# Decoder trunk on one core: the second branch's sums of y formed during the gates and kept in DRAM, one tanh moved, both adds of m ahead of the splits

## The chip, the core and the metric

One core of a Trainium2 chip runs the whole program. The core has five engines that work side by side, each through its own list of instructions in order: TensorE (PE, matrix products), VectorE (DVE), ScalarE (ACT), GpSimd (POOL) and SyncE (SP), which here only issues DMA transfers. SBUF is the on-chip memory, PSUM the small memory into which PE writes its products, and DRAM (HBM) lies outside. The metric is the device time of one execution in microseconds (us); smaller is better.

## What is computed

One layer of a decoder trunk on 1024 positions and 1024 channels, in float32. The part that matters here is the merge of two token mixers:

```python
h = rmsnorm(x, mix_norm[l])
proj = h @ w_in[l]
q, k, v, su, sv, g_a, g_b = jnp.split(proj, splits, axis=-1)
y_att = sliding_window_attention(q, k, v, q_norm[l], k_norm[l], sinks[l])
y_sgu = chunked_spatial_gating(su, sv, sgu_norm[l], w_s[l], b_s[l])
merged = (jax.nn.sigmoid(g_a) * (y_att @ w_oa[l])
          + jax.nn.sigmoid(g_b) * (y_sgu @ w_ob[l]))
x = x + merged @ w_out[l]
x = x + conv_gated_mlp(rmsnorm(x, ffn_norm[l]), w_up[l], conv_w[l], conv_b[l], w_down[l])
```

## The kernel before

**Stages.** The program runs in this order: load and attention (to about 200 us), the spatial gating unit, the *gates* (g_a and g_b, eight pairs of column tiles, to about 380 us), the two branch products with the merge (the *units*, about 380 to 480 us), the product with w_out (to about 560 us), and the MLP.

**Arithmetic.** PE's fast float32 path drops low bits, so each operand is split into a high part (a copy by ACT into type fp32r, `copy_hi`, line 89) and a low part (operand minus high part, on DVE or POOL), and a product is three matmuls: high by high, high by low, low by high. On top of this the large products use a scheme of seven block products instead of eight: the right operand, here y, is cut into four blocks B11, B12, B21, B22, and sums T1 to T4 of these blocks are formed; the seven products are A11·B11, S3·T3, A12·B21, S1·T1, A22·T4, S2·T2 and S4·B22. T1 = B11 - B12, T3 = B12 - B22, T2 = -T1 - B22, T4 = B21 + T2.

**The two y.** Branch "b" is the gating unit, and its y lies in SBUF as `uT`. Branch "a" is attention, and its y lies in DRAM (`d_ya`) and is loaded by `ya_load` into the tile `ya`. `y_sum` (from line 1186) forms one sum of a branch; `y_split` (line 1200) splits one block or sum into the tiles y0 to y6. The sums of "b" are formed in the gates, one for each pair c = 3 to 6 (`gate_pair`); those of "a" are formed in place in `ya`, by `a_begin`, at the end of unit 0.

**The gates.** `gate_pair(c, prev)` makes columns c of g_b and g_a: seven products of 12 matmuls each, with the loads and splits of the weights of the next pair between them. Each gate is scaled (line 1076), goes through tanh on ACT (`gate_out`, line 1089) into a tile `th`, and is stored to DRAM (`dth`), since SBUF has no room for all sixteen.

**The units.** Eight units, in the order of `B_UNITS`: b0, b1, a0, b2, a1, b3, a2, a3. Here they are called unit 0 to unit 7. Unit u is two jobs: the first has the products A11·B11, S3·T3, A12·B21, S1·T1, the second A22·T4, S2·T2, S4·B22, of 6 matmuls each. In between, in this order on each engine:

- ACT copies the first product out of PSUM (`x1`, line 1287), since A12·B21 is added onto the same PSUM bank, and then S3·T3 (`x7`, line 1289). A12·B21 waits for `x1`.
- `hooks` (u, 0) and (u, 1) are pieces of work for branch "a" that are put behind the first and the second job of a unit; the hook "end" (`gates_end`) stands in the first job of unit 0, behind its copies.
- In the second job DVE adds x1 (line 1308), ACT copies the result to `u2` (line 1309), and DVE forms the rest.
- The result times (1 + tanh) goes to a tile `m` for branch "b" (line 1321), and in place for "a" (line 1323). For branch "a" `m_add` then adds it to m (line 1342) and splits m into `mh` and `ml`; it runs behind the first job of the next unit (`late`).
- `run_jobs` splits the weights of job i + 2 (`branch_split`: `wjh` on ACT, line 89, and `wjl` on POOL, line 1273) and loads those of job i + 4 while job i runs; `th_load(u + 1)` loads the two gates of the next unit.

All of this stands in program order (`manual_schedule`), so the order of the lists is the order of the code. Tiles of one tag share a slot or a ring of slots; a new tile waits until the old one's readers are done.

Of the kernel before, what the change touches and what calls it, by code (L numbers as in the profile page):

```python
# [41 lines left out]
def body(ctx, tc, nc, a):  # L42
# [1058 lines left out]
    def gates_close():  # L1101
        pools["gp_cm"].__exit__(None, None, None)
        zr_cm[0].__exit__(None, None, None)
        del pools["AX"]
        pools["mg_cm"] = tc.tile_pool(name="mg", bufs=1)
        pools["mg"] = pools["mg_cm"].__enter__()
        pools["mr_cm"] = tc.tile_pool(name="mr", bufs=1, side="right", reuse_waits="tile")
        pools["mr"] = pools["mr_cm"].__enter__()
        pools["mh0"] = pools["mr"].tile([128, 4, 1024], R, name="mh0")
        pools["mr"].tile([128, 96], F, name="pad_m")  # L1110

    def gate_pair(c, prev):
        w = g_left[c]
        nx = g_left[c + 1] if c < 7 else None
        q = Blocks(w.w, xb)
        x1, x7, q.u2 = q.temps()
        prev.last_sum()
        q.prod(q.g0, "A11", "B11")
        if nx:
            nx.load_q()  # L1120
        else:
            job_load(0)
            job_load(1)
        nc.scalar.copy(x1, q.g0)
        if c == 1:
            gate_out(("a", 0), prev.zv)
        w.split_r()
        gate_out(("b", c - 1), prev.zg)
        if nx:
            wb_add(c - 1)  # L1130
        if 2 < c < 7:
            y_sum("b", ("T1", "T3", "T2", "T4")[c - 3])
        q.prod(q.v0, "S3", "T3")
        nc.scalar.copy(x7, q.v0)
        if not nx:
            y_split("b", "B11")
            y_split("b", "T3")
        q.prod(q.g0, "A12", "B21", more=True)
        if nx:
            nx.sums_q()  # L1140
            nx.split_p()
            nx.split_s3()
        else:
            job_split(0)
            job_load(2)
        q.prod(q.g1, "S1", "T1")
        sub(nc.vector, x7, x7, q.g1)
        if nx:
            nx.sums_r()
        else:  # L1150
            y_split("b", "B21")
            y_split("b", "T1")
        q.prod(q.v0, "A22", "T4", more=True)
        if nx:
            nx.split_q()
        else:
            job_split(1)
        if c == 5:
            ya_load()
        if c < 6:  # L1160
            g_left[c + 2].load_p()
        q.prod(q.v1, "S2", "T2")
        q.sums(x1, x7, q.v0)
        if not nx:
            y_split("b", "T4")
            y_split("b", "T2")
            job_load(3)
        gate_out(("a", c), q.zv)
        q.prod(q.g1, "S4", "B22", more=True)
        if not nx:  # L1170
            y_split("b", "B22")
        return q
# [12 lines left out]

    def y_sum(br, n):

        into = {"a": {"T1": "B11", "T3": "B12", "T2": "B22", "T4": "B21"}, "b": {"T4": "B12"}}[br].get(n)
        if into:
            out = y_src(br, into)  # L1190
        else:
            out = pools["ls"].tile([128, 2, 512], F, tag="m", name=nm("yt"), bufs=3)
        x, y = {"T1": ("B11", "B12"), "T3": ("B12", "B22"), "T2": ("T1", "B22"), "T4": ("B21", "T2")}[n]
        x, y = y_src(br, x), y_src(br, y)
        if n == "T2":
            neg_sum(out, x, y)
        else:
            sub(nc.vector, out, x, y, ALU.add if n == "T4" else ALU.subtract)
        y_raw[br, n] = out

    def y_split(br, n, eng=nc.vector):
        i, j = Y_PLACE[br + n]
# [12 lines left out]
    def gates():  # L1215
        q = v_end()
        for c in range(1, 8):
            q = gate_pair(c, q)
        un["hooks"]["end"] = lambda: gates_end(q)
        un["hooks"][0, 0] = lambda: [y_split("a", n) for n in ("B11", "B22", "B21")]  # L1220
        un["hooks"][0, 1] = a_begin
        un["hooks"][1, 0] = a_end

    def gates_end(q):
        q.last_sum()
        gate_out(("b", 7), q.zg)
        gates_close()
        th_load(0)

    def a_begin():  # L1230
        for n in ("T1", "T3", "T2", "T4"):
            y_sum("a", n)
        y_split("a", "T3")
        y_split("a", "T1")

    def a_end():
        y_split("a", "T4")
        y_split("a", "T2", nc.gpsimd)

    B_UNITS = [("b", 0), ("b", 1), ("a", 0), ("b", 2), ("a", 1), ("b", 3), ("a", 2), ("a", 3)]  # L1240
    ms = {}
# [91 lines left out]
    def m_add(u, j, q):  # L1333

        i = j // 2
        if mhi[i] is None:
            mhi[i] = Y("mh") if i else pools["mh0"]
            mlo[i] = Y("ml")
        for e, z in enumerate((q.zg, q.zv)):
            c = 2 * j + e  # L1340
            m, h, l = ms.pop(c), mhi[i][:, c % 4, :], mlo[i][:, c % 4, :]
            nc.vector.tensor_tensor(m, m, z, op=ALU.add)
            copy_hi(h, m)
            if u == 7 or e == 0:
                nc.vector.tensor_tensor(l, m, h.bitcast(F), op=ALU.subtract)
            else:
                m_lo(m, h, l, L)()
                lo_late.append(m_lo(m, h, l, H))
# [669 lines left out]
```

## Time and profile before

| | us |
|---|---|
| median of three runs | 1202.72 (1202.1 to 1203.13) |
| the profiled execution, its own time | 1203.1 |
| span of its trace (first to last instruction) | 1201.4 |
| PE busy in it | 1173.8 (98%) |
| DVE, ACT, POOL busy | 873.2, 565.6, 620.0 |
| PE busy from 240 to 380 us (gates) | 140.00 of 140 |
| PE busy from 380 to 480 us (units) | 85.06 of 100 |
| PE busy from 580 to 987 us (most of the MLP) | 406.97 of 407 |

The profiled execution is 0.4 us above the median, and 1.7 us of its time lie outside the span. In the rows of a timeline the columns are start, duration, engine, line, operation, output <- inputs by the program's names without buffer numbers, shape, count; in square brackets stands how long the engine had been idle before, and what ended that. PEclk is the clock that PE was granted, 1.00 or 9 in a digit being full speed.

### The profile page before, as it was taken

What the parts mean: (1) busy time and instruction counts of PE and PEld (TensorE: products, weight loads), DVE (VectorE), ACT (ScalarE), POOL (GpSimd) and SP (SyncE); (2) the same over time, 40 slices, a digit from 0 to 9 for tenths busy, and PEclk for the clock granted to TensorE, in tenths of its full rate; (3) what the DMA queues carried; (4) which work ended last, traced back from release to release, by engine and by line L of the source; (5) the groups of instructions that cost most, each with busy time, mean ns of one, the idle gap of its engine ahead of it and who ended that gap; (6) DMA issues with size and microseconds to landing.
All of it is one profiled execution on the core that took longest, in us unless ns stands there. A gap on an engine that the chain in (4) does not pass through costs nothing.

```text
span 1201.4 us, 15911 instructions
## 1 busy us (share of the span) xinstructions
PE 1173.8 (98%) x5842; PEld 991.5 (83%) x5842; DVE 873.2 (73%) x1038; ACT 565.6 (47%) x878; POOL 620.0 (52%) x433
## 2 busy tenths in 40 slices
PE   8999999999999699999999999999999999999998
PEld 8989989888887577788888888888888888888887
DVE  7799966742436767668787878878887798876674
ACT  8555567743336344333644444454444445424331
POOL 2367684588683355344876776767777551000000
PEclk9999999999999799999999999999999999999999
DMA  7010145245654565354564464545545358975471
GB/s 278 26 54 19 53 141 211 89 131 150 174 176 133 172 204 189 92 184 133 130 176 123 140 166 130 155 119 166 142 148 137 100 195 280 368 251 193 146 230 71
DMA packets 79934, 185.51 MB, mean 154 GB/s; under 512 B 9072, under 2 KB 16496, under 8 KB 79728
## 3 DMA queue, kind: packets, MB, share of 16 engines
q1 hardware_dynamic: 72144, 164.57, 40.3%
q0 software_dynamic: 7456, 15.73, 8.4%
q10 hardware_dynamic: 256, 4.19, 1.1%
q8 instruction: 46, 0.75, 0.3%
q14 instruction: 32, 0.26, 0.1%
HBM read 145.40 MB, written 47.45 MB: 161 GB/s over the span
## 4 chain that ended last, share of the span: by engine, by line
PE 59%; DVE 0%; POOL 0%; issue 0%; POOLq 0%
PE pz L1060 35%; PE pd L1832 10%; PE pdy L1832 8%; PE px L95 2%; PE px L94 2%; PE px L93 2%; DVE res L1852 0%; PE pz L140 0%; PE pz L1503 0%; POOL ml L1351 0%; POOL wjl L110 0%; POOLq L110 0%
## 5 line engine op out<-in xcount | busy, mean ns | idle before, releaser
L1060 PE MATMUL pz<-T,qh 128*128 128x512 f32 x472 | 145.6, 390 | 0.0
L1060 PE MATMUL pz<-B,ph 128*128 128x512 f32 x352 | 109.6, 393 | 0.0
L1060 PEld LDWEIGHTS pz<-T,qh 128*128 128x128 f32 x472 | 88.5, 188 | 18.7 <-ACT u L885 0.3
L1019 POOL TENSOR_TENSOR pl<-lp,ph 128x1024 fp32r<-128x1024 f32 x30 | 73.0, 2435 | 52.2 <-ACT ph L89 52.2
L1060 PE MATMUL pz<-T,ql 128*128 128x512 f32 x236 | 91.8, 389 | 0.0
L1060 PE MATMUL pz<-y,wjh 128*128 128x512 f32 x224 | 71.9, 403 | 14.9 <-ACT x L1287 14.8
L1019 POOL TENSOR_TENSOR ql<-lq,qh 128x1024 fp32r<-128x1024 f32 x30 | 76.7, 2556 | 9.1 <-ACT qh L89 9.1
L1060 PEld LDWEIGHTS pz<-B,ph 128*128 128x128 f32 x352 | 65.1, 188 | 15.8 <-ACT x L1672 2.8
L1076 DVE TENSOR_TENSOR pz<-pz,rstd_b 128x1024 f32<-128x1024 f32 x60 | 73.9, 1232 | 4.6 <-ACT rstd_b L143 2.5
L1060 PE MATMUL pz<-T,s3h 128*128 128x512 f32 x232 | 71.4, 389 | 0.0
L1060 PE MATMUL pz<-B,pl 128*128 128x512 f32 x176 | 68.6, 390 | 0.0
L1832 PE MATMUL pd<-bl,ah 128*128 128x512 f32 x176 | 68.5, 389 | 0.0
L1832 PE MATMUL pd<-bh,ah 128*128 128x512 f32 x176 | 68.5, 389 | 0.0
L1832 PE MATMUL pd<-bh,al 128*128 128x512 f32 x176 | 68.5, 389 | 0.0
L1060 PEld LDWEIGHTS pz<-y,wjh 128*128 128x128 f32 x224 | 42.9, 194 | 26.4 <-ACT x L1287 16.5
L1060 PE MATMUL pz<-T,AX 128*128 128x512 f32 x264 | 63.4, 389 | 0.0
L1060 PE MATMUL pz<-B,AX 128*128 128x512 f32 x264 | 63.4, 389 | 0.0
L1273 POOL TENSOR_TENSOR wjl<-wj,wjh 128x512 fp32r<-128x512 f32 (+1 forms) x32 | 36.8, 1170 | 49.2 <-ACT wjh L89 49.2
L622 DVE TENSOR_TENSOR x<-x,pz 128x512 f32<-128x512 f32 x36 | 24.5, 681 | 46.8 <-PE pz L1060 46.8
L1060 PEld LDWEIGHTS pz<-T,AX 128*128 128x128 f32 x264 | 49.6, 188 | 10.3
L1060 PEld LDWEIGHTS pz<-B,AX 128*128 128x128 f32 x264 | 49.6, 188 | 10.3
L1019 POOL TENSOR_TENSOR s3l<-lq,s3h 128x512 fp32r<-128x512 f32 x20 | 25.9, 1297 | 61.5 <-ACT s3h L89 61.5
(353 smaller groups left out, 3601.0 us busy)
## 6 DMA issues: line engine op xcount, KB each, us to landing
lp<-wup SPq DMA_DIRECT2D x22, 512.0 KB, 3.8
lq<-wup SPq DMA_DIRECT2D x22, 512.0 KB, 4.2
ra<-wdown SPq DMA_DIRECT2D x44, 256.0 KB, 4.9
b<-T SPq DMA_DIRECT2D x44, 256.0 KB, 3.5
lq<-wup POOLq DMA_DIRECT2D x42, 256.0 KB, 5.3
B<-tv SPq DMA_DIRECT2D x33, 256.0 KB, 2.0
T<-tt SPq DMA_DIRECT2D x33, 256.0 KB, 2.2
b<-B SPq DMA_DIRECT2D x33, 256.0 KB, 3.0
```

The lines of the kernel that those rows point to most:

```text
L93: nc.tensor.matmul(out, wh, mh, start=first, stop=False, **kw)
L94: nc.tensor.matmul(out, wh, ml, start=False, stop=False, **kw)
L95: nc.tensor.matmul(out, wl, mh, start=False, stop=last, **kw)
L622: eng.tensor_tensor(out, x, y, op=op)
L1019: nc.gpsimd.tensor_tensor(l, r, h.bitcast(F), op=ALU.subtract)
L1060: nc.tensor.matmul(o, p[:, k, :], m, start=not more and k == 0 and j == 0, stop=k == nk - 1 and j == 2, skip_group_check=True)
L1076: nc.vector.tensor_tensor(z, z, rstd_b, op=ALU.mult)
L1273: nc.gpsimd.tensor_tensor(l[:, k], r[:, k], h[:, k].bitcast(F), op=ALU.subtract)
L1832: nc.tensor.matmul(o[d], p[:, k - k0, m], q[:, k - k0, :], start=new and k == 0 and j == 0, stop=k == HK - 1 and j == 2, skip_group_check= ...
```

## The change

The edits, all between the gates and the product with w_out:

1. The sums of branch "a" are formed in the gates. `ya_load` is called in pair c = 1 instead of c = 5, and a table `Y_SUMS` names which sum is made at which of two places of which pair: place 0 is where the sums of "b" stood, place 1 is behind the subtraction of S1·T1 from x7. T3 of "a" is formed in place in `ya`; T1, T2 and T4 are formed in the tiles `yt` (three slots, those that `m` uses later) and stored to DRAM, 512 KB each. Two sums of "b" stay at place 0 and two go to place 1.
2. `ta_load`, at the end of `gates_end`, loads T1, T4 and T2 of "a" from DRAM into a tile `ta`, in the slot in which `mh0` follows later. On SP's list these three loads stand ahead of the gates of unit 0 (`th_load(0)`).
3. The splits of "a" are put elsewhere: behind the first job of unit 0 stand B11 (low part on DVE), B21 and B22 (low parts on POOL, were on DVE), behind its second job T3 and T1, behind the first job of unit 1 T4 and T2 (low part on POOL, as before).
4. The tanh of the last g_a pair (`gate_out(("a", 7))`) goes from the end of the last gate pair to `gates_end`, behind the copies x1 and x7 of unit 0.
5. `m_add` adds both tiles to m before it copies the first high part.

ACT at the start of the units, before (`th` is the tanh of a gate, `y3<-uT` the copy of block B22 of "b", `x1`, `x7`, `u2` the copies of units 0 and 1, `wjh` weights, `y4<-ya` the copies of T3 and T1 of branch "a"; between the two pieces lie weights' high parts and the copies of B11, B22 and B21 of "a"):

```order
L1089 ACTIVATE th_516_4073<-pz_499_3936 128x1024
L89 ACTIVATE y3_518_4089<-uT_59_683 128x1024
L1287 COPY x1_521_4094<-pz_519_4092 128x512
L1289 COPY x7_522_4095<-pz_520_4093 128x512
L1089 ACTIVATE th_524_4125<-pz_498_3935 128x1024
...
L1309 COPY u2_523_4096<-pz_520_4093 128x512
L89 ACTIVATE wjh_535_4192<-wj_515_4069 128x512
L89 ACTIVATE wjh_535_4192<-wj_515_4069 128x256
L89 ACTIVATE y4_539_4207<-ya_476_3764 128x1024 x2
L1287 COPY x1_542_4214<-pz_540_4212 128x512
```

The same place of ACT with the change:

```order
L89 ACTIVATE y3_519_4098<-uT_59_683 128x1024
L1298 COPY x1_522_4103<-pz_520_4101 128x512
L1300 COPY x7_523_4104<-pz_521_4102 128x512
L1089 ACTIVATE th_525_4132<-pz_502_3949 128x1024
L1089 ACTIVATE th_527_4138<-pz_501_3948 128x1024
...
L1320 COPY u2_524_4105<-pz_521_4102 128x512
L89 ACTIVATE wjh_538_4208<-wj_518_4082 128x512
L89 ACTIVATE wjh_538_4208<-wj_518_4082 128x256
L89 ACTIVATE y4_542_4219<-ya_397_3230 128x1024
L89 ACTIVATE y4_542_4219<-ta_4150 128x1024
L1298 COPY x1_545_4226<-pz_543_4224 128x512
```

The first tanh has gone behind x7, and the last of the copies ahead of unit 1's x1 now reads `ta`, which a DMA fills, instead of `ya`.

DVE from the subtraction into x7 of unit 0 to the addition of x1 of unit 1, before (`ya<-ya` are the sums, `y<-ya` the low parts):

```order
L622 TENSOR_TENSOR x7_522_4095<-x7_522_4095,pz_519_4092 128x512
L1208 TENSOR_TENSOR y6_531_4155<-ya_476_3764,y6_531_4155 128x1024 x2
L1208 TENSOR_TENSOR y3_518_4089<-ya_476_3764,y3_518_4089 128x1024
L1308 TENSOR_TENSOR pz_520_4093<-x1_521_4094,pz_520_4093 128x512
...
L1321 SCALAR_TENSOR_TENSOR m_538_4201<-th_527_4141,pz_520_4093 128x1024
L622 TENSOR_TENSOR ya_476_3764<-ya_476_3764 128x2x512 x2
L626 SCALAR_TENSOR_TENSOR ya_476_3764<-ya_476_3764 128x2x512
L622 TENSOR_TENSOR ya_476_3764<-ya_476_3764 128x2x512
L1208 TENSOR_TENSOR y4_539_4207<-ya_476_3764,y4_539_4207 128x1024 x2
L622 TENSOR_TENSOR x7_543_4215<-x7_543_4215,pz_540_4212 128x512
L1208 TENSOR_TENSOR y5_548_4255<-ya_476_3764,y5_548_4255 128x1024
L1308 TENSOR_TENSOR pz_541_4213<-x1_542_4214,pz_541_4213 128x512
```

and with the change:

```order
L622 TENSOR_TENSOR x7_523_4104<-x7_523_4104,pz_520_4101 128x512
L1226 TENSOR_TENSOR y6_534_4171<-ya_397_3230,y6_534_4171 128x1024
L1319 TENSOR_TENSOR pz_521_4102<-x1_522_4103,pz_521_4102 128x512
...
L1332 SCALAR_TENSOR_TENSOR m_541_4217<-th_530_4157,pz_521_4102 128x1024
L1226 TENSOR_TENSOR y4_542_4219<-ya_397_3230,y4_542_4219 128x1024
L1226 TENSOR_TENSOR y4_542_4219<-ta_4150,y4_542_4219 128x1024
L622 TENSOR_TENSOR x7_546_4227<-x7_546_4227,pz_543_4224 128x512
L1226 TENSOR_TENSOR y5_551_4267<-ta_4150,y5_551_4267 128x1024
L1319 TENSOR_TENSOR pz_544_4225<-x1_545_4226,pz_544_4225 128x512
```

The four sums and two of the low parts have left DVE's list here.

SP at the end of the gates with the change (`dth` are the stores of the last two gates, `ta` the new loads, `th` the gates of unit 0, `wj` weights of unit 2):

```order
L1091 DMA dth_526_4134<-th_525_4132 128x1024
L1091 DMA dth_528_4140<-th_527_4138 128x1024
L1216 DMA ta_4150<-taT1_3350 128x1024
L1216 DMA ta_4150<-taT4_3574 128x1024
L1216 DMA ta_4150<-taT2_3487 128x1024
L1262 DMA th_529_4155<-dth_388_3159 128x1024
L1262 DMA th_530_4157<-dth_408_3296 128x1024
L1276 DMA wj_531_4159<-wb 128x256
```

Before, the two `th` loads followed the two stores directly. The diff:

```diff
@@ -1106,8 +1106,6 @@
         pools["mg"] = pools["mg_cm"].__enter__()
         pools["mr_cm"] = tc.tile_pool(name="mr", bufs=1, side="right", reuse_waits="tile")
         pools["mr"] = pools["mr_cm"].__enter__()
-        pools["mh0"] = pools["mr"].tile([128, 4, 1024], R, name="mh0")
-        pools["mr"].tile([128, 96], F, name="pad_m")
 
     def gate_pair(c, prev):
         w = g_left[c]
@@ -1128,8 +1126,7 @@
         gate_out(("b", c - 1), prev.zg)
         if nx:
             wb_add(c - 1)
-        if 2 < c < 7:
-            y_sum("b", ("T1", "T3", "T2", "T4")[c - 3])
+        y_sums(c, 0)
         q.prod(q.v0, "S3", "T3")
         nc.scalar.copy(x7, q.v0)
         if not nx:
@@ -1145,6 +1142,7 @@
             job_load(2)
         q.prod(q.g1, "S1", "T1")
         sub(nc.vector, x7, x7, q.g1)
+        y_sums(c, 1)
         if nx:
             nx.sums_r()
         else:
@@ -1155,7 +1153,7 @@
             nx.split_q()
         else:
             job_split(1)
-        if c == 5:
+        if c == 1:
             ya_load()
         if c < 6:
             g_left[c + 2].load_p()
@@ -1165,7 +1163,8 @@
             y_split("b", "T4")
             y_split("b", "T2")
             job_load(3)
-        gate_out(("a", c), q.zv)
+        if nx:
+            gate_out(("a", c), q.zv)
         q.prod(q.g1, "S4", "B22", more=True)
         if not nx:
             y_split("b", "B22")
@@ -1185,7 +1184,7 @@
 
     def y_sum(br, n):
 
-        into = {"a": {"T1": "B11", "T3": "B12", "T2": "B22", "T4": "B21"}, "b": {"T4": "B12"}}[br].get(n)
+        into = {"a": {"T3": "B12"}, "b": {"T4": "B12"}}[br].get(n)
         if into:
             out = y_src(br, into)
         else:
@@ -1197,6 +1196,25 @@
         else:
             sub(nc.vector, out, x, y, ALU.add if n == "T4" else ALU.subtract)
         y_raw[br, n] = out
+        if br == "a" and n != "T3":
+            d = d_ta[n] = pools["dr"].tile([128, 1024], F, tag=f"ta{n}", name=f"ta{n}")
+            nc.sync.dma_start(d, out.rearrange("p a b -> p (a b)"))
+
+    d_ta = {}
+    Y_SUMS = {(2, 1): "aT1", (3, 0): "aT3", (3, 1): "aT2", (4, 0): "aT4", (4, 1): "bT1", (5, 0): "bT3",
+              (5, 1): "bT2", (6, 0): "bT4"}
+
+    def y_sums(c, e):
+        n = Y_SUMS.get((c, e))
+        if n:
+            y_sum(n[0], n[1:])
+
+    def ta_load():
+        t = pools["mr"].tile([128, 4, 1024], F, tag="mh0", name="ta")
+        pools["mr"].tile([128, 96], F, name="pad_m")
+        for i, n in enumerate(("T1", "T4", "T2")):
+            nc.sync.dma_start(t[:, i, :], d_ta[n])
+            y_raw["a", n] = t[:, i, :].rearrange("p (a b) -> p a b", a=2)
 
     def y_split(br, n, eng=nc.vector):
         i, j = Y_PLACE[br + n]
@@ -1217,25 +1235,18 @@
         for c in range(1, 8):
             q = gate_pair(c, q)
         un["hooks"]["end"] = lambda: gates_end(q)
-        un["hooks"][0, 0] = lambda: [y_split("a", n) for n in ("B11", "B22", "B21")]
-        un["hooks"][0, 1] = a_begin
-        un["hooks"][1, 0] = a_end
+        un["hooks"][0, 0] = lambda: (y_split("a", "B11"), y_split("a", "B21", nc.gpsimd),
+                                     y_split("a", "B22", nc.gpsimd))
+        un["hooks"][0, 1] = lambda: (y_split("a", "T3"), y_split("a", "T1"))
+        un["hooks"][1, 0] = lambda: (y_split("a", "T4"), y_split("a", "T2", nc.gpsimd))
 
     def gates_end(q):
+        gate_out(("a", 7), q.zv)
         q.last_sum()
         gate_out(("b", 7), q.zg)
         gates_close()
+        ta_load()
         th_load(0)
-
-    def a_begin():
-        for n in ("T1", "T3", "T2", "T4"):
-            y_sum("a", n)
-        y_split("a", "T3")
-        y_split("a", "T1")
-
-    def a_end():
-        y_split("a", "T4")
-        y_split("a", "T2", nc.gpsimd)
 
     B_UNITS = [("b", 0), ("b", 1), ("a", 0), ("b", 2), ("a", 1), ("b", 3), ("a", 2), ("a", 3)]
     ms = {}
@@ -1334,12 +1345,14 @@
 
         i = j // 2
         if mhi[i] is None:
-            mhi[i] = Y("mh") if i else pools["mh0"]
+            mhi[i] = Y("mh") if i else pools["mr"].tile([128, 4, 1024], R, tag="mh0", name="mh0")
             mlo[i] = Y("ml")
         for e, z in enumerate((q.zg, q.zv)):
             c = 2 * j + e
+            nc.vector.tensor_tensor(ms[c], ms[c], z, op=ALU.add)
+        for e in (0, 1):
+            c = 2 * j + e
             m, h, l = ms.pop(c), mhi[i][:, c % 4, :], mlo[i][:, c % 4, :]
-            nc.vector.tensor_tensor(m, m, z, op=ALU.add)
             copy_hi(h, m)
             if u == 7 or e == 0:
                 nc.vector.tensor_tensor(l, m, h.bitcast(F), op=ALU.subtract)
```

## The prediction

> **What bounds the kernel now.** I read the page first, then the waits of PE, then the timeline of each engine where PE waits.
>
> ```profile
> span 1201.4 us, 15911 instructions
> ...
> PEclk9999999999999799999999999999999999999999
> ```
>
> PE is the bound nearly everywhere: only what PE loses can be won. The clock digits show one fall, in the fourteenth slice, at about 400 us. The list of waits for PE from 376 to 420 us and from 420 to 480 us names the same line both times (columns: total, count, longest):
>
> ```profile
> PE pz L1060 <- ACT x L1287: 12.4, 2, 11.1
> ```
> ```profile
> PE pz L1060 <- ACT x L1287: 2.4, 2, 1.2
> ```
>
> So 14.8 us go in four waits for one thing, the copy x1 that ACT makes in the first job of a unit. In the timeline of PE the two early ones are these:
>
> ```profile
> 383.78 0.73 PE L1060 MATMUL pz<-y,wjh 128*128 128x512 f32 x2 [1.23 <-ACT x L1287]
> ...
> 393.23 0.39 PE L1060 MATMUL pz<-y,wjl 128*128 128x512 f32 x1
> 404.76 1.22 PE L1060 MATMUL pz<-y,wjh 128*128 128x512 f32 x2 [11.15 <-ACT x L1287]
> ...
> 417.20 0.62 PE L1060 MATMUL pz<-y,wjh 128*128 128x512 f32 x2
> ```
>
> They are the A12·B21 of units 0, 1 and 2; unit 2's came without a wait. After the long wait the matmuls themselves were slow. Stretches of the window view (length, PE, PEld, DVE, ACT, POOL, granted clock):
>
> ```profile
> 404.76:410.70 5.94, 5.93 (x14) 4.68 (x15) 2.58 (x3) 1.23 (x3) 0.08 (x1) 0.50 0.05 19
> 410.70:417.20 6.50, 6.50 (x29) 5.33 (x29) 4.76 (x6) 4.16 (x7) 6.50 (x4) 1.00 0.20 61
> ```
>
> For 5.94 us a matmul took 0.424 us instead of 0.224, so 14 of them cost 14 x 0.200 = 2.8 us more. The long wait is worth 11.15 + 2.8 = 14 us, over 1% of the time.
>
> Why x1 of unit 1 was late, by ACT's timeline:
>
> ```profile
> 381.28 1.03 ACT L1089 ACTIVATE th<-pz 128x1024 f32<-128x1024 f32 x1 [0.86 <-DVE pz L1076]
> 382.21 1.05 ACT L89 ACTIVATE y<-uT 128x1024 fp32r<-128x1024 f32 x1
> 383.15 0.58 ACT L1287 COPY x<-pz 128x512 f32<-128x512 f32 x1
> ...
> 386.55 1.03 ACT L1089 ACTIVATE th<-pz 128x1024 f32<-128x1024 f32 x1 [2.33 <-DVE pz L1076]
> 387.47 1.14 ACT L89 ACTIVATE wjh<-wj 128x512 fp32r<-128x512 f32 x2
> 388.51 2.95 ACT L89 ACTIVATE y<-ya 128x1024 fp32r<-128x1024 f32 x3
> 394.71 0.58 ACT L1309 COPY u<-pz 128x512 f32<-128x512 f32 x1 [3.26 <-DVE pz L1308]
> 395.20 0.94 ACT L89 ACTIVATE wjh<-wj 128x512 fp32r<-128x512 f32 x2
> 402.24 2.00 ACT L89 ACTIVATE y<-ya 128x1024 fp32r<-128x1024 f32 x2 [6.11 <-DVE ya L622]
> 404.15 0.56 ACT L1287 COPY x<-pz 128x512 f32<-128x512 f32 x1
> ```
>
> x1 (404.15) stands behind two copies of branch "a" that waited 6.11 us for sums on DVE, and those behind u2, which waited 3.26 us for DVE's line 1308. DVE at that time:
>
> ```profile
> 389.59 4.48 DVE L1208 TENSOR_TENSOR y<-ya,y 128x1024 fp32r<-128x1024 f32 x3 [1.95 <-ACT y L89]
> 394.00 0.68 DVE L1308 TENSOR_TENSOR pz<-x,pz 128x512 f32<-128x512 f32 x1
> ...
> 397.46 2.35 DVE L1321 SCALAR_TENSOR_TENSOR m<-th,pz 128x1024 f32<-128x1024 f32 x2
> 399.73 2.48 DVE L622 TENSOR_TENSOR ya<-ya 128x1024 f32<-128x1024 f32 x2
> ```
>
> **Unit 0: the tanh behind the copies.** Without the tanh at 381.28 the copy of B22 and x1 (383.15) come up to 1.03 us earlier, x1 ending by 382.8 at the latest. PE was ready at 383.78 - 1.23 = 382.55, so at most 0.3 of this wait stays, and PE comes to unit 1's wait about 1.2 us sooner, at 393.62 - 1.2 = 392.4. Alone this wins nothing, since ACT's x1 of unit 1 does not hang on it. The second tanh (386.55) waited for DVE, and the first now fits into the 2.33 us of idle time before it.
>
> **Unit 1: x1 comes earlier in two steps.** The row at 389.59 has three low parts; only the first stays on DVE. Three at a mean of 1.49 against about 1.22 for one undisturbed; I leave the whole excess to the first and take off the other two, 2 x 1.14 (their ends overlap) = 2.25. So line 1308, u2 and the weights' copies come 2.25 sooner. Next, the two copies no longer wait for sums on DVE: 402.24 becomes 395.20 + 0.94 = 396.14, another 6.1. x1 goes from 404.15 to 404.15 - 8.35 = 395.8, and A12·B21 of unit 1 from 404.76 to 396.4. If the first low part should cost 1.22 only, it is 0.8 less still; if a copy waits for something new, more (below).
>
> The new thing is T1 of "a", which ACT copies at 396.14 - 2.25 + 1.0 = 394.9 out of a tile that a DMA fills. The SP queue before, and the time from issue to landing of the first of the `th` loads at 388.01 and of the first at 392.29:
>
> ```profile
> 388.01 1.20 SPq L1251 DMA_DIRECT2D th<-dth  x2
> 389.31 2.94 SPq L1265 DMA_DIRECT2D wj<-wb  x4
> 392.29 0.91 SPq L1251 DMA_DIRECT2D th<-dth  x2
> ```
> ```profile
> th<-dth SPq DMA_DIRECT2D x1, 512.0 KB, 5.8
> ```
> ```profile
> th<-dth SPq DMA_DIRECT2D x1, 512.0 KB, 5.5
> ```
>
> T1's load takes the place of the first `th`, right behind the same store, with the same size: it lands at 388.01 + 5.8 = 393.8, 1.1 us ahead of its use. The cover is thin.
>
> **The gap that stays, and the clock.** PE stands still from 392.4 to 396.4, 4.0 us. Before, the fall to 0.50 came within the 11.15 us and lasted to 5.94 us after its end; the three waits of 1.2 us drew none in the digits. A stop of 4.0 us lies between. I take it as not falling in two cases of three; if it falls, it costs what it cost before, 2.8. The Trainium skill, page "TensorE: Matmul & The Clock Gate", section "What's actually happening", says that the clock halves after an idle window of about 3.4 us, and that these windows run free of the kernel. By that rule a stop of 4.0 us would hold a whole window in about (4.0 - 3.4)/3.4, or one case of six (an estimate); no run here shows a stop of this length yet.
>
> At this point the gain is 404.76 - 396.4 = 8.4, plus 2.8 of clock: 11.2.
>
> **Unit 2: what is late next.** The gates of unit 0 now come behind three loads of 512 KB. Before, a store, two `th` and four weight loads (2 MB in all) went ahead of the `th` at 392.29, which landed at 392.29 + 5.5 = 397.8; now a store and three loads, 2 MB too, go ahead of the first `th` of unit 0. So DVE's line 1321, which would be free at about 395.2 (397.46 - 2.25), starts at 397.8 and ends at 397.8 + 2.35 = 400.2. Behind it stand, before u2 of unit 1: the low parts of T3 and T1 (1.22 each), the x7 sum (0.69), T4 (1.22) and line 1308 (0.68), 5.0 us; then on ACT u2 (0.58), weights (0.94) and x1 of unit 2 (0.56): 407.3 at best. DVE and POOL disturb each other where both subtract in SBUF:
>
> ```profile
> 412.04 2.22 DVE L1208 TENSOR_TENSOR y<-ya,y 128x1024 fp32r<-128x1024 f32 x1 [1.00 <-ACT y L89]
> ```
> ```profile
> 413.13 3.40 POOL L1208 TENSOR_TENSOR y<-ya,y 128x1024 fp32r<-128x1024 f32 x1
> ```
>
> The low part of T4 took 2.22 instead of 1.22 there. With the change three such DVE subtractions run while POOL has two pieces of weights and T2's low part: none to all three are held, 0 to 3.6 us (the longest by a whole POOL subtraction of 2.4). I take two at 1.0, the size measured: x1 of unit 2 ends at 409.3. PE is there at 396.4 + 7 products x 6 x 0.226 = 405.9, so a gap of 3.4 us opens (1.4 to 5.0) where before there was none. A12·B21 of unit 2 goes from 417.20 to 409.3: 7.9 us won up to here. The Trainium skill, page "SBUF — State Buffer", section "Who interferes with whom", says that a DVE instruction with two SBUF inputs and a POOL instruction that reads SBUF exclude each other for a whole instruction. The rows agree (2.22 - 1.22 = 1.0); if the two alternate strictly here, the sum loses the 3.6 and not 2.0.
>
> **The adds of m.** In units 3 and 5 line 1308 came behind the second add, which came behind the first split:
>
> ```profile
> 433.87 1.22 DVE L1342 TENSOR_TENSOR m<-m,pz 128x1024 f32<-128x1024 f32 x1
> 435.00 0.69 DVE L1308 TENSOR_TENSOR pz<-x,pz 128x512 f32<-128x512 f32 x1
> ```
>
> The second add fits into the time in which DVE waits for the first high part, so line 1308 stands 1.13 sooner (435.00 to 433.87), and with it u2 and x1 of the next unit. The waits were 1.2: at most 0.1 each stays. The second high part on ACT comes sooner too and leaves u2's way. Gain 2.2 to 2.4; I take 2.4.
>
> **The gates.** Four more sums fall to DVE (1.22, up to 2.2 if disturbed) at place 1. DVE and POOL have this idle time in each pair:
>
> ```profile
> 358.11 0.69 DVE L1069 TENSOR_TENSOR pz<-x,pz 128x512 f32<-128x512 f32 x1 [4.68 <-PE pz L1060]
> ```
> ```profile
> 308.11 2.40 POOL L1019 TENSOR_TENSOR gax<-lr,gax 128x1024 fp32r<-128x1024 f32 x1 [4.59 <-ACT gax L89]
> ```
>
> A sum in the 4.68 us ahead of line 1069 delays nothing, and POOL can lose 1.0 twice out of 4.59. The three stores and the four loads of `ya`, now in pair 1, go where PE is far ahead of no transfer. Cost 0, down to no gain either; if the cover failed, each sum would cost at most 2.2, 9 us in all.
>
> **Sum.** 1203.1 (this execution) - 7.9 - 2.4 = 1192.8. Against the median, 0.4 lower, 1192.4. I predict 1192.6.
>
> **Rivals.**
>
> *The clock falls in one of the gaps*: 1192.6 + 2.8 = 1195.4. For it: each gap is near the length that must decide. Against: nothing between 1.2 and 11.15 is seen here. Chance 0.22.
>
> *DVE and POOL alternate strictly* (the mechanism above): 1.6 more, 1194.2. Chance 0.12.
>
> *The second gap closes*: if the `th` of unit 0 land as they did for 397.46 and DVE is not held, x1 of unit 2 ends before 405.9 and all 3.4 stay: 1189.2. Against: three loads ahead. Chance 0.12.
>
> *T1's load replaces the sums as the wait*: the six transfers share the engines instead of going in order, and T1 lands with the last, at 398. x1 comes 3.1 later, the gap of 7 us draws the clock down (2.8), the second gap shrinks by up to 3.1: 1195.4 to 1198.5. The spread of landings speaks against it. Chance 0.07.
>
> *Slower*: one wait, ACT in front of `ta` T1, so long that it eats all. With the second gap gone (3.4) and the clock lost (2.8) break-even is a landing at 394.9 + 10.3 + 3.4 - 2.8 = 405.8, 17.8 us after issue, three times the 5.8 measured; at 20 us, 1205. Chance 0.03.
>
> Forecast: 0.44. **Numbers**: the range holds forecast, clock, alternation and closed gap with their bounds, 1188.8 to 1197.2. A difference under 0.2% (2.4 us) can't be told from none. All cases but the last are faster by more; I leave 0.02 for a landing between: faster 0.95, same 0.02, slower 0.03.
>
> **What would show it.** The sums at lines 622 and 626 gone from 399 to 405; x1 of unit 1 near 395.8; PE's waits for x1 at two places, 3 to 5 and 1 to 5 us, and none behind the adds of m; line 1321 of unit 0 released by a DMA; clock 1.00 at 400 us; no wait of PE in the gates. Wrong if ACT waits for `ta`, if PE waits in the gates, or if the clock row shows 0.50.

## The result, and the profile after

The change is faster: 1190.86 us (median of four runs, 1190.21 to 1192.38) against 1202.84 us before (four runs beside them), a ratio of 0.9903, 95% interval 0.9886 to 0.992. In the four series of experiments the kernel before stood at 1202.4 to 1203.5 us. The forecast was 1192.6 us, with a range of 1188.8 to 1197.2.

The page of the changed kernel, its first line and its clock digits:

```profile
span 1188.5 us, 15919 instructions
...
PEclk9999999999999999999999999999999999999999
```

The span is 12.9 us shorter, and the fall of the clock at 400 us no longer reaches a digit. The waits of PE, from 376 to 420 us and from 420 to 480 us (total, count, longest):

```profile
PE pz L1060 <- ACT x L1298: 4.2, 1, 4.2
```
```profile
PE pz L1060 <- ACT x L1298: 0.2, 1, 0.2
```

Of 14.8 us, 4.4 are left. Where PE stands still, and unit 2's A12·B21, in its timeline:

```profile
391.97 0.39 PE L1060 MATMUL pz<-y,wjl 128*128 128x512 f32 x1
396.57 1.22 PE L1060 MATMUL pz<-y,wjh 128*128 128x512 f32 x2 [4.22 <-ACT x L1298]
...
407.59 0.61 PE L1060 MATMUL pz<-y,wjh 128*128 128x512 f32 x2
```

Unit 1 still has its gap; unit 2 at 407.59 has none, so the second gap that the forecast had is missing. That first row has two matmuls in 1.22 us where 0.61 is usual: the clock did fall. Windows of this stretch (length, PE, PEld, DVE, ACT, POOL, granted clock, DMA share, GB/s), and the gates:

```profile
392.35:396.00 3.65, 0.00 (x1) 0.00 (x0) 2.34 (x4) 3.27 (x6) 3.65 (x2) 1.00 1.01 378
396.00:399.50 3.50, 2.93 (x7) 2.35 (x8) 1.88 (x2) 1.01 (x3) 2.55 (x3) 0.51 0.96 322
399.50:403.00 3.50, 3.50 (x16) 2.89 (x16) 3.45 (x5) 2.20 (x4) 1.49 (x1) 1.00 1.05 404
```
```profile
240.00:380.00 140.00, 140.00 (x619) 115.66 (x618) 64.38 (x68) 60.19 (x76) 108.84 (x67) 1.00 0.56 168
```

One stretch of 3.4 us ran at half clock, and only its part with PE at work cost time: its seven matmuls, 7 x 0.227 = 1.6 us at full clock, took 2.93. With the eighth, which starts in it, the loss is about 1.4 us. The gates lost nothing.

ACT on the way to x1 of unit 1 and of unit 2:

```profile
392.73 0.59 ACT L1320 COPY u<-pz 128x512 f32<-128x512 f32 x1 [0.99 <-DVE pz L1319]
393.22 0.94 ACT L89 ACTIVATE wjh<-wj 128x512 fp32r<-128x512 f32 x2
394.06 1.05 ACT L89 ACTIVATE y<-ya 128x1024 fp32r<-128x1024 f32 x1
395.00 1.04 ACT L89 ACTIVATE y<-ta 128x1024 fp32r<-128x1024 f32 x1
395.95 0.57 ACT L1298 COPY x<-pz 128x512 f32<-128x512 f32 x1
...
405.23 0.59 ACT L1320 COPY u<-pz 128x512 f32<-128x512 f32 x1 [1.37 <-DVE pz L1319]
405.71 0.94 ACT L89 ACTIVATE wjh<-wj 128x512 fp32r<-128x512 f32 x2
406.55 0.58 ACT L1298 COPY x<-pz 128x512 f32<-128x512 f32 x1
```

x1 of unit 1 starts at 395.95 (forecast 395.8), with nothing ahead of it that waits: T1's copy at 395.00 has no bracket, its load, the first of the three, having landed at 388.30 + 5.3 = 393.6:

```profile
388.30 2.33 SPq L1216 DMA_DIRECT2D ta<-taT  x3
```
```profile
ta<-taT SPq DMA_DIRECT2D x1, 512.0 KB, 5.3
```

DVE and POOL behind it:

```profile
397.62 2.41 DVE L1332 SCALAR_TENSOR_TENSOR m<-th,pz 128x1024 f32<-128x1024 f32 x2 [2.24 <-DMA th<-dth]
399.94 1.22 DVE L1226 TENSOR_TENSOR y<-ya,y 128x1024 fp32r<-128x1024 f32 x1
401.07 1.22 DVE L1226 TENSOR_TENSOR y<-ta,y 128x1024 fp32r<-128x1024 f32 x1
402.21 0.68 DVE L622 TENSOR_TENSOR x<-x,pz 128x512 f32<-128x512 f32 x1
402.94 1.59 DVE L1226 TENSOR_TENSOR y<-ta,y 128x1024 fp32r<-128x1024 f32 x1
404.46 0.68 DVE L1319 TENSOR_TENSOR pz<-x,pz 128x512 f32<-128x512 f32 x1
```
```profile
401.51 4.17 POOL L1284 TENSOR_TENSOR wjl<-wj,wjh 128x512 fp32r<-128x512 f32 x2 [2.96 <-ACT wjh L89]
```

Line 1332 (1321 before) waits for its gate's load and starts at 397.62, forecast 397.8. But of its three low parts only the last is held, by 0.37 us; the two pieces of weights on POOL, 2.56 us before (at 410.62), took 4.17 in the same time. So x1 of unit 2 ended at 407.13, 0.46 us before PE came.

### The profile page after: what moved, and what is told of

The parts are those of the page before. It is cut to its first block, busy times and chain, and to the rows that moved or that the text cites. A ratio compares the mean times of both kernels' runs of the same rounds, so it can differ in the third digit from the quotient of the medians.

```text
span 1188.5 us, 15919 instructions
## 1 busy us (share of the span) xinstructions
PE 1171.1 (99%) x5842; PEld 990.9 (83%) x5842; DVE 874.2 (74%) x1036; ACT 566.4 (48%) x878; POOL 630.9 (53%) x435
## 4 chain that ended last, share of the span: by engine, by line
PE 85%; DVE 6%; issue 2%; ACT 2%; POOL 1%; DMA 0%; SPq 0%; ACTq 0%; POOLq 0%; DVEq 0%
PE pz L1060 52%; PE pd L1845 10%; PE pdy L1845 8%; PE px L95 2%; PE px L94 2%; PE px L93 2%; PE pq L93 1%; PE pq L95 1%; PE pq L94 1%; PE pv L519 1%; DVE xa L622 1%; PE pu L95 1%; PE pu L93 1%; PE pu L94 1%; DVE y L1226 0%
## 5 line engine op out<-in xcount | busy, mean ns | idle before, releaser
L1060 PEld LDWEIGHTS pz<-T,AX 128*128 128x128 f32 x264 | 49.6, 188 | 10.3
L1060 PEld LDWEIGHTS pz<-B,AX 128*128 128x128 f32 x264 | 49.6, 188 | 10.3
L1540 DVE SCALAR_TENSOR_TENSOR tg<-pz,cp,tg 128x1023 f32<-128x1023 f32 (+1 forms) x44 | 56.2, 1278 | 0.8
L1540 DVE SCALAR_TENSOR_TENSOR tv<-pz,cp,tv 128x1023 f32<-128x1023 f32 (+1 forms) x44 | 56.2, 1278 | 0.8
```

Of the source, the lines that this page charges most:

```text
L1060: nc.tensor.matmul(o, p[:, k, :], m, start=not more and k == 0 and j == 0, stop=k == nk - 1 and j == 2, skip_group_check=True)
L1540: nc.vector.scalar_tensor_tensor(t[:, j:], p[:, 0:1024 - j], cw[:, ci, 2 - j:3 - j], t[:, j:], op0=ALU.mult, op1=ALU.add)
```

## The experiments

Two executions of one kernel can differ by a row of half clock, so besides the ratio to before (with its interval) the table has a length from the profiled execution: from the last u2 copy of the gates (line 1070) to the sixteen small matmuls of line 140, behind all units, PE's work between them being the same in all. Outside this stretch the profiled executions differ too, by up to 2.3 us (span less stretch: 992.3 before, 992.5 in the change, 994.6 in e7, whose edit lies inside the stretch). Its two rows, of before and of the change:

```profile
377.93 0.59 ACT L1070 COPY u<-pz 128x512 f32<-128x512 f32 x1 [2.75 <-DVE pz L1069]
...
587.04 1.95 PE L140 MATMUL pz<-ident,ss8b 128*128 128x128 f32 x16
```
```profile
378.22 0.59 ACT L1070 COPY u<-pz 128x512 f32<-128x512 f32 x1 [2.75 <-DVE pz L1069]
...
574.20 1.95 PE L140 MATMUL pz<-ident,ss8b 128*128 128x128 f32 x16
```

The runs are named by the number that their labels begin with.

| run | ratio to before | stretch, us | PE's wait at unit 1 | half-clock rows of 3.41 us at the units |
|---|---|---|---|---|
| before | 1 | 209.11 | 11.15 | 4 |
| the change | 0.9903 (0.9886 to 0.992) | 195.98 | 4.22 | 1 |
| e11, the change again | 0.9904 (0.989 to 0.9919) | 197.38 | 4.21 | 2 |
| e1 | 0.9967 (0.9954 to 0.9979) | 205.53 | 11.15 | 4 |
| e2 | 0.9925 (0.9913 to 0.9938) | 200.52 | 4.18 | 2 |
| e3 | 0.9906 (0.9892 to 0.9919) | 196.17 | 2.67 | 1 |
| e4 | 0.9912 (0.9897 to 0.9927) | 197.47 | 5.16 | 1 |
| e5 | 0.9925 (0.991 to 0.994) | 199.41 | 6.46 | 2 |
| e6 | 0.9956 (0.994 to 0.9973) | 203.78 | 10.80 | 4 |
| e7 | 0.9898 (0.9883 to 0.9913) | 195.77 | 2.30 | 0 |
| e8 | 0.9894 (0.9879 to 0.9909) | 195.04 | 2.32 | 0 |
| e9 | 0.9877 (0.9861 to 0.9893) | 194.52 | 0.25 | 0 |
| e10 | 0.9901 (0.9884 to 0.9917) | 197.06 | 0.24 | 1, at unit 2 |

### The adds of m, alone and undone

In `m_add` of the kernel before:

```diff
+            nc.vector.tensor_tensor(ms[c], ms[c], z, op=ALU.add)
+        for e in (0, 1):
+            c = 2 * j + e
             m, h, l = ms.pop(c), mhi[i][:, c % 4, :], mlo[i][:, c % 4, :]
-            nc.vector.tensor_tensor(m, m, z, op=ALU.add)
             copy_hi(h, m)
```

> The kernel before, with only the second add of m put ahead of the first split. Theory (the prediction's term): the two waits of PE for x1 behind the adds of m shrink from 1.2 us each to at most 0.1, so the time falls by 2.2 to 2.4 us, to about 1200.4. Rival: the waits go, but the high parts, now later by one add, hold the weights' copies or the next unit's products, and PE loses it again there: no change within 0.5 us.

The second run takes the same edit back in the changed kernel.

> The changed kernel, with the adds of m as they were before. Theory: the two waits of 1.2 us return, +2.2 to +2.4 us, about 1193.1. Rival: in the changed kernel the weights of these jobs come later and the adds no longer decide: within 0.5 us of 1190.9.

Alone the edit brought 0.33% (0.0033 x 1203.5 = 4.0 us; in the stretch 3.6, of which 0.3 lie ahead of the first add). Undone it cost 0.9925 - 0.9903 = 0.22%, 2.6 us; in the stretch 200.52 - 197.38 = 3.1 us against e11, which has as many rows at half clock. So it is more than the 2.4 us of the waits in PE's list. PE's timeline of before, around the first of them, and of e1 at the same place:

```profile
434.65 0.39 PE L1060 MATMUL pz<-y,wjl 128*128 128x512 f32 x1
435.15 0.72 PE L1060 MATMUL pz<-y,wjh 128*128 128x512 f32 x2
...
436.40 0.40 PE L1060 MATMUL pz<-y,wjl 128*128 128x512 f32 x1
438.02 0.74 PE L1060 MATMUL pz<-y,wjh 128*128 128x512 f32 x2 [1.22 <-ACT x L1287]
```
```profile
436.65 0.39 PE L1060 MATMUL pz<-y,wjl 128*128 128x512 f32 x1
437.24 0.72 PE L1060 MATMUL pz<-y,wjh 128*128 128x512 f32 x2 [0.20 <-ACT x L1287]
```

Matmuls follow each other every 0.227 us (three in 0.68). From 436.40 to 438.02 are 1.62 us, so the stop shown as 1.22 cost 1.39: the list counts from the modelled end of a matmul, 0.39 us after its start, and not from when the next could have started. And the step from 434.65 to 435.15 hides a stop of 0.27 with no bracket at all. In this unit 1.39 + 0.27 = 1.66 us were lost before, and 0.59 - 0.23 = 0.36 in e1.

Comparing the starts of the same matmuls in the kernel before and in e1, the gain is 2.8 us at the two places of the list, and another 0.4 comes at a third that has no bracket either, at the head of the product with w_out, before:

```profile
482.84 0.39 PE L93 MATMUL px<-mh,wjh 128*128 128x512 f32 x1
483.37 0.50 PE L94 MATMUL px<-ml,wjh 128*128 128x512 f32 x1
```

These two starts are 0.53 us apart instead of 0.23. By the chain of releases the second waited for POOL's last low part of `ml` (line 1351, 482.06 to 483.32), which stands behind the last add of m. In e1 and with the change the step is gone.

### The tanh back in place

In the changed kernel, as in the runs that follow where nothing else is said:

```diff
-        if nx:
-            gate_out(("a", c), q.zv)
+        gate_out(("a", c), q.zv)
...
     def gates_end(q):
-        gate_out(("a", 7), q.zv)
```

> The changed kernel, with the last tanh of branch a back ahead of the copy of B22. Theory (the prediction: alone it wins nothing): a wait of about 1.2 us returns at unit 0, PE comes 1.2 us later to unit 1's wait for x1, which ends where it ended, so that gap shrinks from 4.2 to about 3.0 us. The gap is then shorter than the 3.41 us of one row of the clock, no whole row can be idle, and the clock does not fall (1.4 us won); PE then waits for x1 of unit 2 by what it came earlier, about 0.9 us. In all 0 to -0.5 us. Rival: the tanh holds x1 of unit 1 too or the gap keeps its length, so that the wait is lost time: +1.2 us.

The wait of 1.23 us at unit 0 returned and the gap at unit 1 fell to 2.67 (about 3.0 expected):

```profile
394.24 0.39 PE L1060 MATMUL pz<-y,wjl 128*128 128x512 f32 x1
397.30 1.22 PE L1060 MATMUL pz<-y,wjh 128*128 128x512 f32 x2 [2.67 <-ACT x L1296]
```

The time is that of the change (0.9906 against 0.9903; the stretch 0.2 us longer). So the tanh's move alone wins nothing measurable. But the clock fell after a gap of 2.67 us: that half of the expectation was wrong.

### The gates' loads first

```diff
-        ta_load()
         th_load(0)
+        ta_load()
```

> The changed kernel, with the loads of unit 0's gates issued ahead of the three loads of a's sums. Theory (the cover of T1's load is thin, 1.1 us): T1 lands 1.4 to 2.8 us later, ACT's copy of it waits for the DMA, x1 of unit 1 ends 1.5 to 2 us later, and the gap and the clock take more; line 1321 of unit 0 starts earlier than 397.6. In all +1 to +3 us. Rival: the transfers share the engines, T1 lands hardly later, and the earlier gates are a gain: 0 to -1 us.

ACT now waits for T1's load:

```profile
395.86 1.06 ACT L89 ACTIVATE y<-ta 128x1024 fp32r<-128x1024 f32 x1 [0.86 <-DMA ta<-taT]
```

x1 ends 0.9 us later and the gap is 5.16 us; the ratio is 0.0009 higher (1.1 us), inside the intervals, and the stretch 1.5 us longer than that of the change with as many rows at half clock (1). T1's load is thus not the wait in the change, but two loads ahead of it make it one.

### The low parts back on DVE

```diff
-        un["hooks"][0, 0] = lambda: (y_split("a", "B11"), y_split("a", "B21", nc.gpsimd),
-                                     y_split("a", "B22", nc.gpsimd))
+        un["hooks"][0, 0] = lambda: (y_split("a", "B11"), y_split("a", "B21"),
+                                     y_split("a", "B22"))
```

> The changed kernel, with the low parts of B21 and B22 back on DVE, as before. Theory (the prediction's first step at unit 1, 2.25 us): line 1319 and u2 come 2.2 us later, x1 of unit 1 ends about 2.2 us later, the gap is about 6.4 us and the clock stays low one row of 3.41 us longer (up to 1.5 us); a little of it is taken back at unit 2. +2 to +4 us. Rival: u2 and the weights' copies were not what x1 stood behind, and the loads of a's sums decide: 0 to +0.5 us.

```profile
395.94 0.58 ACT L1320 COPY u<-pz 128x512 f32<-128x512 f32 x1 [3.26 <-DVE pz L1319]
...
399.15 0.57 ACT L1298 COPY x<-pz 128x512 f32<-128x512 f32 x1
```

u2 waits 3.26 us for DVE, as it did before. From the last u2 of the gates (379.16 in this run) to x1 are 19.99 us, against 17.73 in the change: 2.26 later, and the gap is 6.46. The ratio is 0.9925, 2.6 us slower. The term of 2.25 us stands.

### The sums back in unit 0

The kernel before, with the tanh and the adds as in the change, and the low parts too:

```diff
-        un["hooks"][0, 0] = lambda: [y_split("a", n) for n in ("B11", "B22", "B21")]
+        un["hooks"][0, 0] = lambda: (y_split("a", "B11"), y_split("a", "B21", nc.gpsimd),
+                                     y_split("a", "B22", nc.gpsimd))
         un["hooks"][0, 1] = a_begin
```

> The kernel before, with the tanh moved, the two low parts on POOL and the adds of m ahead, but with a's sums formed in unit 0 and kept in SBUF, as before. Theory (the prediction: 6.1 of the 8.4 us at unit 1 come from the sums that leave): only the 2.25 us of the low parts and what the adds bring (2.4 predicted, 3 to 3.6 in the run with the adds alone) are won, and ACT still waits some 6 us for line 622 ahead of x1: about 1197 to 1198.5. Rival: with the low parts on POOL the sums fit where DVE waited, and x1 comes nearly as early as in the changed kernel: about 1191 to 1193.

1198.15 us, 0.9956: as the theory had it.

```profile
392.97 0.58 ACT L1312 COPY u<-pz 128x512 f32<-128x512 f32 x1 [0.99 <-DVE pz L1311]
...
400.90 2.00 ACT L89 ACTIVATE y<-ya 128x1024 fp32r<-128x1024 f32 x2 [6.51 <-DVE ya L622]
```

u2 comes as early as in the change, and then ACT waits 6.51 us for the sums. The stretch is 203.78 - 195.98 = 7.8 us longer than with all of the change: the sums' leaving is its largest part.

### Further work behind x1

In e7, with a new hook in a unit's first job, behind x1 and x7:

```diff
-        un["hooks"][0, 1] = lambda: (y_split("a", "T3"), y_split("a", "T1"))
+        un["hooks"][1, "mid"] = lambda: (y_split("a", "T3"), y_split("a", "T1"))
...
-        ta_load()
         th_load(0)
+        ta_load()
...
+            un["hooks"].get((u, "mid"), lambda: None)()
             yield
```

In e8 beside it:

```diff
-        un["hooks"][1, 0] = lambda: (y_split("a", "T4"), y_split("a", "T2", nc.gpsimd))
+        un["hooks"][2, "mid"] = lambda: (y_split("a", "T4"), y_split("a", "T2", nc.gpsimd))
```

> The changed kernel, with the copies and low parts of T3 and T1 of branch a put behind x1 of unit 1 instead of ahead of it, and the loads of unit 0's gates ahead of those of a's sums. Theory (what is left of the gap at unit 1 is ACT's order: two copies of 1.0 us stand ahead of x1): x1 of unit 1 starts at about 394.0 instead of 395.95, PE's gap shrinks from 4.2 to about 2.2 us, x1 of unit 2 comes about as early as PE: -1 to -2.5 us, about 1189. Rival: DVE's and ACT's work is only moved behind x1 and makes x1 of unit 2 late by as much: within 0.5 us of 1190.9.

> As the run e7_t3_t1_behind, and also the copies and low parts of T4 and T2 of branch a behind x1 of unit 2. Theory: u2 of unit 1 and x1 of unit 2 come 2 us or more earlier than there, so that no wait of PE is left at unit 2; against the changed kernel -2 to -3.5 us, about 1187.5 to 1189. Rival: the products that read T4 and T2 then wait for the copies, a wait of 1 us or more with another releaser than x1, and it is no faster than e7_t3_t1_behind.

The gap fell to 2.30 and 2.32 us in the two, as expected, and the clock stayed at 1.00. The time did not follow: 0.9898 and 0.9894 against 0.9903 can't be told apart, and the stretch is 0.2 and 0.9 us shorter. The waits of PE in e8, 376 to 420 us:

```profile
PE pz L1060 <- ACT x L1298: 2.5, 2, 2.3
PE pz L1060 <- DVE x L622: 0.8, 1, 0.8
PE pz L1060 <- POOL y L1226: 0.4, 1, 0.4
```

Four short stops stand where one was: 3.7 us in the list, and some 0.2 us more for each, while the change loses 4.2 + 0.2 + 1.4. The new wait for line 622 is DVE's: the low parts of T3 and T1 now stand ahead of the subtraction that frees a PSUM bank. In e7 there are three stops, the third of them x1 of unit 2 again, 1.54 us. Both forecast gains were too high by this, and the rival of e7, a time within 0.5 us of the change, holds.

### A version meant to beat both

The hooks of e9 at units 0 and 1; the one of T4 and T2 stays as in e8, and `ta_load()` leaves `gates_end` (`y_hi` is the copy of `y_split`, `y_lo` its low part):

```diff
+        un["hooks"][0, 0] = lambda: (ta_load(), y_split("a", "B21", nc.gpsimd), y_hi("a", "B22"))
+        un["hooks"][0, 1] = lambda: y_lo("a", "B22", nc.gpsimd)
+        un["hooks"][1, "mid"] = lambda: [y_hi("a", n) for n in ("B11", "T3", "T1")]
+        un["hooks"][1, 0] = lambda: (y_lo("a", "B11"), y_lo("a", "T3"), y_lo("a", "T1", nc.gpsimd))
```

> A version meant to beat both: as e8_all_behind, but B11's copy and low part of branch a, which held line 1319 and u2 of unit 0, go behind x1 of unit 1 too; the low part of B22 on POOL goes behind the next weights, T1's low part to POOL, and the loads of a's sums behind the weights of unit 1. Theory (the gap of 2.3 us at unit 1 that e7_t3_t1_behind and e8_all_behind still have is DVE's 2.2 us on B11 ahead of line 1319): u2 of unit 0 starts at about 390.8 instead of 392.7, x1 of unit 1 at about 392.1, the gap shrinks to 0.6 us or less, the clock does not fall; against the changed kernel -2 to -4 us, about 1187 to 1189. Rival: the work moved behind x1 of unit 1 is late for unit 2's products or for x1 of unit 2, and a wait of 1.5 us or more stands there instead: within 0.5 us of e8_all_behind.

1188.99 us, 0.9877 (0.9861 to 0.9893), the lowest of all, at the upper end of what was expected; its interval, from another chip, overlaps that of the change. The gap at unit 1 is 0.25 us, and no row is at half clock. The rival holds in part: x1 of unit 2 now waits behind weights whose load is late, and PE waits 0.83 us at 401.89 and 0.34 us at 411.08 for low parts on POOL.

```profile
406.12 0.72 PE L1060 MATMUL pz<-y,wjh 128*128 128x512 f32 x2 [1.66 <-ACT x L1304]
```
```profile
398.69 1.06 ACT L89 ACTIVATE y<-ta 128x1024 fp32r<-128x1024 f32 x1 [2.59 <-DMA ta<-taT]
...
404.66 0.94 ACT L89 ACTIVATE wjh<-wj 128x512 fp32r<-128x512 f32 x2 [2.67 <-DMA wj<-wb]
```

### T1's copy and the last loads later

The same hooks in e10 (`ta_load` takes the names to load):

```diff
+        un["hooks"][0, 0] = lambda: (ta_load(["T1"]), y_split("a", "B21", nc.gpsimd), y_hi("a", "B22"))
+        un["hooks"][0, 1] = lambda: (ta_load(["T4", "T2"]), y_lo("a", "B22", nc.gpsimd))
+        un["hooks"][1, "mid"] = lambda: [y_hi("a", n) for n in ("B11", "T3")]
+        un["hooks"][1, 0] = lambda: (y_lo("a", "B11"), y_lo("a", "T3"), y_split("a", "T1", nc.gpsimd))
```

> As e9_first_sum_first, but the copy of T1 of branch a goes behind the weights' copies of unit 2 on ACT, where the wait for its load (2.59 us) held these, and the loads of T4 and T2 go behind the weights of unit 2's second job, which ACT waited 2.67 us for ahead of x1 of unit 2. Theory: the waits of PE at 401.9 (0.83, weights) and 406.1 (1.66, x1) go, with what a stop costs beside its wait (0.3 to 0.4 us each): -2 to -3 us against e9_first_sum_first, about 1186 to 1187. Rival: T4 and T2 then come too late for the products that read them, and a wait of 1 us or more for them takes back half or more: 1188 to 1189.

> The changed kernel as it is, on the same chip as e10_t1_later, so that the two can be compared directly: 0.990 of before, as measured. If the clock's fall in the gap comes and goes by the phase of its 3.41 us rows, the profile shows one or two such rows at half clock again, or none; none expected at the gap's 4.2 us.

e10 is no better than the change on the same chip (0.9901 against 0.9904): the rival's mechanism holds, and at 1191.2 us it cost more than the 1188 to 1189 that it was priced at. The wait at 401.9 went and the one of x1 shrank to 1.08, but T4's low part came too late and was held besides:

```profile
410.39 0.53 PE L1060 MATMUL pz<-y,wjh 128*128 128x512 f32 x1 [3.02 <-DVE y L1231]
```
```profile
407.13 3.20 DVE L1231 TENSOR_TENSOR y<-ta,y 128x1024 fp32r<-128x1024 f32 x1
```
```profile
406.90 2.35 POOL L1231 TENSOR_TENSOR y<-ta,y 128x1024 fp32r<-128x1024 f32 x1
```

The low part takes 1.22 us by itself and 3.20 here. POOL's subtraction began 0.23 us ahead of it and ended at 409.25; 409.25 + 1.22 = 410.47, about where DVE's ended (410.33): DVE waited for all of POOL's instruction. e11, the change itself, had two rows at half clock where its first profile had one, and a stretch 1.4 us longer for it; none had been expected.

## Why the prediction was right, step by step

The time lies in the range, 1.7 us below the forecast, and the main path, x1 of unit 1, came as worked out. That the forecast is this close is in part luck: the second gap did not open (3.4 us gained), the adds brought more (0.8), and the clock fell (1.4 lost), three departures that partly cancel. One sign of being wrong that the prediction named did come: the granted clock was 0.51 from 396.0 to 399.5 us. And PE's wait for x1 stood at one of the two places forecast.

- **The bound.** Right. All that was won but some 0.4 us at the head of the product with w_out was won where PE waited for x1: the stretch from the gates' end to line 140 fell by 209.11 - 195.98 = 13.1 us, and the gates and the rest stood as they were.
- **Unit 0, the tanh.** Right: the wait went, and e3 shows that alone it is worth nothing (0.9906 against 0.9903).
- **Unit 1, x1.** Right in both parts and in size: 395.95 against 395.8 forecast, with the low parts worth 2.26 (e5, forecast 2.25) and the sums shown as the larger part (e6). T1's load came in time, with 395.00 - 393.6 = 1.4 us to spare (forecast 1.1); e4 shows that the cover is as thin as was said.
- **The gap and the clock.** The gap was 4.22 us (forecast 4.0). This step failed: the forecast took the clock as not falling, and it fell, for one row and not for four, at 1.4 us and not 2.8. Of the seven profiles with a gap of 2.67 to 6.46 us (the change twice, e2, e3, e4, e5, and e10 at unit 2) all seven fell, four of them without a wholly idle row, so the forecast's chance, one in three in the working and 0.22 in the list of rivals, was far too low. By the Trainium skill's rule on a whole idle window (page "TensorE: Matmul & The Clock Gate", section "What's actually happening") the prediction estimated one case in six. The trace of the change fits that rule, since one row was wholly idle; the four others do not.
- **Unit 2.** The other step that failed: no second gap of 3.4 us opened. Line 1321's wait for its load came as forecast (397.62 against 397.8), but the two collisions of 1.0 us each did not: the DVE rows lost 0.37 us in all, and POOL's weights lost 4.17 - 2.56 = 1.6 in their place. The Trainium skill's page "SBUF — State Buffer" (section "Who interferes with whom") has it that the two exclude each other for a whole instruction, and that the one that starts first holds on; this trace and e10 agree. In e10 POOL began first, and here DVE's low part of T1 at 401.07 stood ahead of POOL's weights at 401.51. The forecast had charged every meeting to DVE, though its own POOL row at 413.13, 3.40 us where 2.40 is usual, shows that POOL pays too. This is read from the trace; no run changed it alone. With PE later by 1.4 us of clock besides, x1 came in time: at full clock PE would have come at about 407.6 - 1.4 = 406.2 and waited some 0.9 us for x1's end at 407.13 (an estimate from these rows), so the two departures are not independent. So the 7.9 us became 7.9 + 3.4 (no second gap) - 1.4 (clock) = 9.9, which is what the trace shows: A12·B21 of unit 2, counted from the last u2 of the gates, at 407.59 - 378.22 = 29.37, before 417.20 - 377.93 = 39.27. The rival "the second gap closes" and the rival "the clock falls" came true together.
- **The adds of m.** Right in mechanism, too small in size: 2.4 forecast from the list of waits, 3.1 to 3.3 measured (e2, and e1 without the 0.3 us ahead of its first add). The list under-counts the two stops (2.8 and not 2.4), and the third place, 0.4 us at the head of the product with w_out, was not in the forecast.
- **The gates.** Right: cost nothing, with 140.00 us of PE in 140.

The sum of the terms as measured is 9.9 + 3.2 = 13.1 us, against 10.3 forecast. By the two profiled executions 12.9 us were won, by the medians 12.0: the profiled execution of the change was 0.7 us under its median, that of before 0.3 over.

## What to carry to other kernels

Follow the engine that waits back through what stands ahead in the other engine's list: one 11 us wait here was two copies queued behind a wait of their own, and moving the sums that they waited for was worth more than the rest of the change. A stop costs more than the idle time that the profile lists (about 0.2 us a stop here), and starts of neighbouring instructions show stops that no list has; compare their spacing before a small gain is priced. Where two engines hold each other up, ask which of them begins first before the price is put on one. Work pushed behind one deadline meets the next: e7 and e8 shortened the first gap from 4.2 to 2.3 us, e9 and e10 to 0.2, and most of that came back as waits for DVE, for weights and for a low part, so that only e9 may be faster than the change, and its interval does not settle it.

## What the runs showed of the hardware

**The clock fell after rows that were idle in large part, not only after wholly idle ones.** The trace's clock record at the units is in multiples of 3.413 us (3.413 at half clock in the change, 6.827 in e11, 13.653 before), at a phase that differs from run to run: the first half-clock row begins 17.88 us behind the last u2 of the gates in the change and 17.55 in e11, the same kernel. Idle time of PE by the profile in a row, against the clock in the next row, for the rows with the longest stops at the units:

```
full clock, next row full:   idle 1.58 (e7), 1.66 (e9), 1.76 (e8), 1.85 (e4), 1.90 (e5)
full clock, next row half:   idle 2.06 (e1), 2.42 (e6), 2.51 (e3), 2.83 (e2), 3.02 (e10), 3.31 (e4), 3.41 (before, change, e5, e11)
half clock, next row full:   idle 0 (all others), 0.16 (e3), 0.47 (change)
half clock, next row half:   idle 0.79 (e11), 0.89 (before), 1.14 (e5), 1.35 (e2), 1.55 (e6), 2.27 (e1), 3.41 (before, e1, e6)
```

At the units the clock falls somewhere between 1.90 and 2.06 us of idle time in 3.41, and it comes back after a row with at most 0.47 us of it and not after one with 0.79 or more. So a stop of 2.7 us can draw it down (e3) and one of 2.3 us didn't (e7, e8), and the same kernel loses one row or two by the phase alone (the change and e11). A row costs at most half of 3.41, 1.7 us, and less by what of it is idle.

At the program's start the listed idle time is not a good measure: rows with 1.47 (e4, from 5.02 us), 1.78 (e10), 1.82 (before) and 1.91 us (e7) were followed by half clock. There the matmuls have 256 columns and start up to 0.30 us apart where 0.11 is the closest spacing, so PE is idle between them without a bracket. As an estimate of PE's real work, each matmul can be counted as 0.227 us for 512 columns at full clock, in proportion for fewer, and twice that at half clock. Then one pair of bounds fits every pair of neighbouring rows in the thirteen traces whose clock is recorded: full clock is followed by full up to 2.07 us of idle time and by half from 2.21 on, and half clock by full up to 0.63 and by half from 0.93 on.

**DVE and POOL.** The same kind of meeting went against POOL in the change (4.17 us for 2.56) and against DVE in e10 (3.20 for 1.22). In both the one that had begun went on, and the other ended about a full length of its own later: POOL's first piece of weights (1.28 us by itself) at 403.45, after DVE's end at 402.29, and in e10 DVE's low part at 410.33, after POOL's end at 409.25.
